# The last block's tail of a layer kernel: p's products kept on chip, W_G by blocks of k, weights split anew, one norm moved

## The chip, the cores and the metric

One Trainium2 chip, one core. The metric is the time of one execution on the device in microseconds (us); lower is better. A core has a matrix engine (PE, the tensor engine, with PEld for its weight loads), a vector engine (DVE), a scalar engine (ACT), a general engine (POOL) and SP, which issues transfers. Each works through its own queue in order; they meet at semaphores. Transfers (DMAs) issued by SP and POOL are carried out by 16 DMA engines. PE writes its sums to PSUM banks; all other tiles lie in SBUF; what is spilled lies in HBM.

## The reference

One layer is applied to 2048 prompt tokens and to 64 sample tokens. Only the part ahead of the output is touched by the change:

```python
merged = jax.nn.sigmoid(gA) * yA + jax.nn.sigmoid(gB) * yB
out = jnp.einsum('btd,de->bte', merged, w_o)
x = x + rms_norm(out, g_post)
gate = jax.nn.sigmoid(jnp.einsum('btd,de->bte', rms_norm(x, g_ple), w_ple_gate))
x = x + jnp.einsum('btp,pd->btd', p.astype(x.dtype), w_ple_proj) * gate
return x, new_conv, S_new
```

D_MODEL is 1024 and p has 256 columns. Everything is in float32.

## The kernel before

The 2112 tokens are cut into three blocks of BN = 704, and each block into two halves of HN = 352 (bl["segs"]). Activations lie feature by token: a tile `r` holds 128 features of a block, so eight tiles (KB = 8) make an operand. They come from one ring of 52 tiles (rt).

A float32 product is made of three matmuls in a shorter format: an operand is split into hi (rounded, cast by ACT, L184) and lo (the rest, subtracted by DVE, L185), and hi*hi, hi*lo and lo*hi are added in PSUM (mm3, L468 to L473, its three matmuls at L471, L472, L473). One output tile of 128 features by 352 tokens is thus 8 x 3 = 24 matmuls. split_w does the same for weights, which come as two halves of 128 x 512 each: the raw half is loaded by SP (L195). If its low part was kept in HBM by an earlier block, hi is cast by ACT (L215) and lo is loaded by SP (L216) into one of four tiles `lo` or three tiles `s`; otherwise lo is split by DVE (L185) into one of the four tiles `lo`. There are four tiles `hi` and five tiles `raw`.

In the last block, the stage W_O (out_in_turn) sums squares of its outputs, and its hooks already begin the norm of the first half. Then come:

- ple (L904 to L927): p times w_ple_proj, eight tiles of 2 x 6 matmuls (L918 to L920), copied from PSUM by ACT (L922) to a tile, which POOL spills (L924). After each tile a hook runs.
- final_gate (L1057 to L1069) for the first half, then for the second: per output tile j a product with W_G (gemm), a sigmoid (L1065), a reload of p by POOL (L931), multiply (L1066), add (L1067) and a store of y (L1068; on POOL, for j of 6 and 7 on SP). The reload brings all 704 columns for each half.

final_norm (L1020 to L1055) has 20 steps for one half: 2 for the reciprocal root of the mean square (sums by PE L558, scaling L530 on DVE, power on POOL L532, spread by PE L542, copied by ACT L568), 8 that scale, add x and square (L1040, L1041, L576, L577; x is loaded by POOL, L1032), 2 for the second root, and 8 that scale and split the operand of W_G (L1053, L184, L185). spread_out lays a list of counts over hooks: so many steps of a norm run at each hook. A framework schedules the instructions of one engine among each other from this order and from priorities, so that PE's matmuls of several output tiles can stand interleaved.

The hooks of the last block, before: the first norm runs 5 steps in W_O and 15 in the eight hooks of ple. The second norm runs 2 in ple (its first root) and 18 in the first seven hooks of the first half's gate.

Of the kernel before, what the change touches and what calls it, by code (L numbers as in the profile page):

```python
# [32 lines left out]
W_A, W_B, W_O, W_G = 80, 88, 96, 104  # L33
# [49 lines left out]
def hybrid_step(  # L83
# [17 lines left out]
    V, A, G, T, SP = nc.vector, nc.scalar, nc.gpsimd, nc.tensor, nc.sync  # L101
# [30 lines left out]
    def spill(kind, j):  # L132
        return dram.tile([P, BN], F32, tag=f"{kind}{j}", name=nm(kind), bufs=2)
# [76 lines left out]
    def split_w(raw, key=None):  # L210

        hi = wp.tile([P, 4, P], F32R, tag="hi", name=nm("hi"))
        if key in lows:
            lo = low_tile()
            A.copy(hi, raw)  # L215
            SP.dma_start(lo.bitcast(F32), lows[key])  # L216
            return hi, lo
        lo = wp.tile([P, 4, P], F32R, tag="lo", name=nm("lo"))
        split(raw, hi, lo)
        if key is not None:  # L220
            lows[key] = dram.tile([P, 4, P], F32, tag=f"lo{key}", name=nm("low"), bufs=1)
            SP.dma_start(lows[key], lo.bitcast(F32))
        return hi, lo

    def load_w(idx):

        parts = []
        for half_ in range(2):
            raw = load_raw(w_blk[idx, half_])
            with tc.high_priority():  # L230
                parts.append(split_w(raw, (idx, half_)))
        return parts

    last, hooks = [None], []
# [5 lines left out]
    def hook():  # L240

        if hooks:
            step = hooks.pop(0)
            if step is not None:
                step()
# [222 lines left out]
    def mm3(ps, w, act, k, c):  # L468
        hi, lo = w[k // 4]
        xhi, xlo = act[k]  # L470
        T.matmul(ps, hi[:, k % 4, :], xhi[:, c], start=k == 0, stop=False)  # L471
        T.matmul(ps, hi[:, k % 4, :], xlo[:, c], start=False, stop=False)  # L472
        last[0] = T.matmul(ps, lo[:, k % 4, :], xhi[:, c], start=False, stop=k == KB - 1).ins  # L473

    def cols_of(s):
        return slice(s["off"], s["off"] + s["n"])

    def gemm(idx, act, segs):
        w = load_w(idx)
        outs = []  # L480
        for s in segs:
            ps = ps_gemm()
            for k in range(KB):
                mm3(ps, w, act, k, cols_of(s))
            outs.append(ps)
            hook()
        return outs
# [10 lines left out]
                            mm3(ps, w, act, k, cols_of(s))  # L498
        return pss

    def gemm_by_k(idxs, act, segs):

        ws = [load_w(i) for i in idxs]
        pss = [[ps_gemm() for _ in segs] for _ in idxs]
        for k in range(KB):
            for row, w in zip(pss, ws):
                for ps, s in zip(row, segs):
                    mm3(ps, w, act, k, cols_of(s))
        return pss

    def gemms(idx0, act, segs, by_k=False):
# [394 lines left out]
    def ple(bl, ph, kept):  # L906
        for j in range(KB):
            raw = wp.tile([P, 4, P], F32, tag="raw", name=nm("raw"), bufs=5)[:, :2, :]
            SP.dma_start(raw, w_ple[j])
            with tc.high_priority():  # L910
                hi = wp.tile([P, 4, P], F32R, tag="hi", name=nm("hi"))[:, :2, :]
                lo = wp.tile([P, 4, P], F32R, tag="lo", name=nm("lo"))[:, :2, :]
                split(raw, hi, lo)
            t = rt()
            for s in bl["segs"]:
                pp, c = ps_attn()[:, :HN], cols_of(s)
                for k, (xhi, xlo) in enumerate(ph):
                    T.matmul(pp, hi[:, k, :], xhi[:, c], start=k == 0, stop=False)  # L918
                    T.matmul(pp, hi[:, k, :], xlo[:, c], start=False, stop=False)
                    last[0] = T.matmul(pp, lo[:, k, :], xhi[:, c], start=False, stop=k == 1).ins  # L920
                with tc.high_priority():
                    A.copy(t[:, c], pp)  # L922
            kept["p", j] = spill("p", j)
            G.dma_start(kept["p", j], t)  # L924
            hook()
            yield


    def reload(d):
        t = rt()  # L930
        G.dma_start(t, d)  # L931
        return t
# [121 lines left out]
            split(t[:, c], h2[j][0][:, c], h2[j][1][:, c])  # L1054
            yield  # L1055

    def final_gate(bl, segs, xo, h2, kept):  # L1057
        c = slice(segs[0]["off"], segs[-1]["off"] + HN)
        for j in range(KB):
            pss = gemm(W_G + j, h2, segs)  # L1060
            xj = reload(kept["x", j]) if ("x", j) in kept else xo[j]
            pj = reload(kept["p", j])
            t = rt()
            for s, ps in zip(segs, pss):
                A.activation(t[:, cols_of(s)], ps, AF.Sigmoid)  # L1065
            V.tensor_tensor(t[:, c], pj[:, c], t[:, c], ALU.mult)  # L1066
            V.tensor_tensor(t[:, c], t[:, c], xj[:, c], ALU.add)  # L1067
            (SP if bl["last"] and j >= KB - 2 else G).dma_start(y_fm[j * P : (j + 1) * P, segs[0]["t0"] : segs[0]["t0"] + len(segs) * HN], t[:, c])  # L1068
            yield  # L1069


    def spread_out(*plans):

        for counts in zip_longest(*(plan for _, plan in plans), fillvalue=0):
            todo = [(gen, n) for (gen, _), n in zip(plans, counts) if n]
            hooks.append((lambda todo=todo: [run(gen, n) for gen, n in todo]) if todo else None)
# [25 lines left out]
    for bi, bl in enumerate(blocks):  # L1102
        first, kept = bi == 0, kepts[bi]
        segs = bl["segs"]
        path_b(bl, hc, first, kept, fills)
        run(fills)
        a = []
        nxt = None if bl["last"] else blocks[bi + 1]
        cols, a_first = [], []
        rows = row_rstd(nxt, cols) if nxt else iter(())  # L1110
        sums_ahead = prepare_sums(W_A, W_B) if first else prepare_sums(W_O) if bi == 1 else iter(())

        def side(rows, sums_):
            for j in range(KB):
                if j <= 3:
                    next(rows, None)
                if j >= 3:
                    next(sums_, None)
                yield

        def ready():
            a_first.extend(narrow(half(t, 0)) for t in a[:KH])

        path_a(bl, hc, a, first, side(rows, iter(()) if first else sums_ahead), None if first else ready)
        assert not hooks
        if first:
            next(sums_ahead)
        mg, xo, h2, acc = [], [], [], rt()
        if first:
            mg = merge(bl, a, kept, sums_ahead)  # L1130
        else:
            parts = [None] * KB

            def made(j, h):

                if nxt:
                    if parts[j] is None:
                        parts[j] = rt(dt=F32R), rt(dt=F32R)
                    split(half(mg[j], h), *(half(t, h) for t in parts[j]))

            stages, loads = merge_in_turn(a, kept, mg, made)
            if not nxt:
                stages.append(out_in_turn(mg, xo, acc))
            loads(W_A, -1)
            for idx, n in in_turn(stages, a_first):
                loads(idx, n)
                if (idx, n) == (W_B, 5) and not nxt:
                    ph = [split_rt(raw) for raw in load_p(bl, G)]
                if (idx, n) == (W_O, 4):
                    norms = [final_norm(bl, [s], xo, acc, h2, None) for s in segs]  # L1150
                    spread_out((norms[0], (0, 0, 1, 0, 1, 1, 1, 1)))
            if nxt:
                mg = parts
        if nxt:
            hc = new_operands()
            ops = operands(hc, spread_all(cols), partial(load_x, nxt))
            for j, _ in enumerate(final_out(segs, mg, xo, acc, by_k=True)):
                if j in (1, 3, 5):
                    run(ops, 1)
            run(ops)  # L1160
            fills = gates(nxt, hc, kepts[bi + 1], False)
            norm = final_norm(bl, segs, xo, acc, h2, kept)
            spread_out((norm, (0, 1, 0, 1) + (0, 1, 0) * KB + (1, 0, 1) + (0, 1) * KB))
            run(fills, LEAD)
            assert not hooks
            run(final_gate(bl, segs, xo, h2, kept))
        else:
            gate = [final_gate(bl, [s], xo, h2, kept) for s in segs]
            spread_out((norms[0], (2, 2, 1, 1, 1, 3, 3, 2)), (norms[1], (0, 0, 1, 0, 1, 0, 0, 0) + (3, 3, 2, 1, 1, 4, 4)))
            run(ple(bl, ph, kept))  # L1170
            run(gate[0])
            assert not hooks
            run(gate[1])
# [49 lines left out]
```

## Time and profile before

| what | value |
|---|---|
| runs shown | 2727.76, 2730.09, 2732.46 us; median 2730.09 |
| the profiled execution | 2728.34 us |
| its span, first to last instruction | 2726.6 us |
| mean granted TensorE clock | 0.987 |
| PE busy in the span | 2646.6 us |
| DMA from 2640 to 2720 us | 25.95 MB, mean 324 GB/s |
| a cast of weights, ACT L215, 128 x 512 | 619 ns mean, 740 in the kernel |
| a split of weights, DVE L185, 128 x 512 | 660 ns mean |

The page calls each group of instructions by line, engine, operation and tile: "L347 PE MATMUL pg<-r,lo" is the matmul of line 347 that writes a PSUM tile pg and reads r and lo. In a list of waits, "PE pg L473 <- DMA s<-low: 1.7, 1, 1.7" says that PE's line 473 waited for a transfer to s, 1.7 us in all, once, 1.7 us the longest. In the timeline, a row is start, duration, engine, line, operation and tiles, and in brackets the idle time ahead of it with what ended it. Matmuls overlap: one that lasts 0.32 us lets the next start after 0.16 us. Starts are us from the first instruction.

### The profile page before, as it was taken

To read this page: it belongs to the slowest core of one execution; us is meant where nothing else is said; L and a number is where in the kernel's file an instruction comes from. 1 tells how busy PE (TensorE), PEld (TensorE's weight loads), DVE (VectorE), ACT (ScalarE), POOL (GpSimd) and SP (SyncE) were. 2 spreads that over 40 slices of the span, in tenths; PEclk is the share of its full clock that TensorE was granted. 3 is DMA by queue.
4 is the path that set the end of the run, shared out by engine and by line. 5 is a ranking of instruction groups with operands and counts; after the bars stand their busy time and mean duration, and the time that the engine had idled before them with its cause. 6 is when DMAs were issued, how large, how long until landed. Compare 5 with 4: busy or idle time off the path is not lost.

```text
span 2726.6 us, 47857 instructions
## 1 busy us (share of the span) xinstructions
PE 2646.6 (97%) x16736; PEld 2610.7 (96%) x16736; DVE 1721.8 (63%) x3327; ACT 1457.9 (53%) x2796; POOL 367.9 (13%) x684
## 2 busy tenths in 40 slices
PE   6999999999999999999999999999999999999998
PEld 5999999999999999999999999999999999999988
DVE  6788888899666643566645567554355554357864
ACT  4665565454324553566654556454466654445654
POOL 1000001100332211011111210021010010010022
PEclk7999999999999999999999999999999999999999
DMA  5767777898988898766789998598866678888878
GB/s 200 268 239 275 260 243 278 280 314 291 346 312 288 305 340 271 243 224 223 232 279 335 390 335 259 180 349 306 268 224 219 217 225 269 272 290 305 280 240 313
DMA packets 365681, 748.90 MB, mean 275 GB/s; under 512 B 44704, under 2 KB 48320, under 8 KB 365440
## 3 DMA queue, kind: packets, MB, share of 16 engines
q1 hardware_dynamic: 325728, 589.84, 64.9%
q0 software_dynamic: 39424, 155.96, 15.6%
q8 instruction: 132, 2.16, 0.3%
q14 instruction: 109, 0.89, 0.1%
q10 hardware_dynamic: 288, 0.05, 0.0%
HBM read 538.29 MB, written 207.37 MB: 273 GB/s over the span
## 4 chain that ended last, share of the span: by engine, by line
PE 78%; DMA 8%; DVE 4%; issue 4%; ACT 2%; POOL 1%; SPq 0%; DVEq 0%; POOLq 0%; ACTq 0%
PE pg L345 17%; PE pg L346 17%; PE pg L347 17%; PE pg L472 3%; PE pg L473 3%; PE pg L471 3%; PE pg L438 3%; PE pg L439 3%; PE pg L440 3%; DMA raw<-w_blk 2%; DMA raw<-S 1%; PE pa L826 1%; PE pa L862 1%; PE pa L864 1%; PE pa L816 1%
## 5 line engine op out<-in xcount | busy, mean ns | idle before, releaser
L345 PE MATMUL pg<-r,hi 128*128 128x352 f32 x3360 | 1115.1, 333 | 15.9 <-ACT r L184 5.9
L346 PE MATMUL pg<-r,hi 128*128 128x352 f32 x3360 | 1090.4, 325 | 5.0 <-DVE r L185 5.0
L347 PE MATMUL pg<-r,lo 128*128 128x352 f32 x2400 | 779.9, 325 | 4.8 <-DMA lo<-low 3.5
L215 ACT CAST hi<-raw 128x512 fp32r<-128x512 f32 x740 | 455.9, 619 | 589.7 <-PE pg L346 216.3
L345 PEld LDWEIGHTS pg<-r,hi 128*128 128x128 f32 x3360 | 634.8, 189 | 26.8 <-ACT r L184 8.9
L346 PEld LDWEIGHTS pg<-r,hi 128*128 128x128 f32 x3360 | 635.6, 189 | 9.6 <-DVE r L185 9.5
L347 PEld LDWEIGHTS pg<-r,lo 128*128 128x128 f32 x2400 | 454.0, 189 | 7.0 <-DMA lo<-low 4.7
L347 PE MATMUL pg<-r,s 128*128 128x352 f32 x960 | 310.5, 324 | 0.4 <-DMA s<-low 0.3
L472 PE MATMUL pg<-r,hi 128*128 128x352 f32 x896 | 291.9, 326 | 2.6 <-DVE r L185 2.3
L471 PE MATMUL pg<-r,hi 128*128 128x352 f32 x896 | 290.3, 326 | 1.8 <-ACT r L184 1.7
L473 PE MATMUL pg<-r,lo 128*128 128x352 f32 x728 | 237.5, 326 | 8.3 <-DVE lo L185 7.2
L184 ACT CAST r<-r 128x352 fp32r<-128x352 f32 (+2 forms) x294 | 162.8, 589 | 144.0 <-DVE r L962 43.3
L184 ACT CAST hi<-raw 128x512 fp32r<-128x512 f32 (+1 forms) x232 | 138.1, 597 | 181.2 <-PE pg L346 44.1
L185 DVE TENSOR_TENSOR r<-r,r 128x352 fp32r<-128x352 f32 (+2 forms) x294 | 183.6, 650 | 60.7 <-ACT r L184 60.0
L185 DVE TENSOR_TENSOR lo<-raw,hi 128x512 fp32r<-128x512 f32 (+1 forms) x232 | 152.2, 660 | 73.2 <-ACT hi L184 66.8
L438 PE MATMUL pg<-r,hi 128*128 128x352 f32 x560 | 182.6, 330 | 7.9 <-ACT r L184 7.9
L439 PE MATMUL pg<-r,hi 128*128 128x352 f32 x560 | 183.9, 330 | 0.9 <-DVE r L185 0.6
L347 PEld LDWEIGHTS pg<-r,s 128*128 128x128 f32 x960 | 180.4, 188 | 1.3 <-DMA s<-low 1.3
L472 PEld LDWEIGHTS pg<-r,hi 128*128 128x128 f32 x896 | 169.9, 190 | 4.5 <-DVE r L185 4.3
L184 ACT CAST hi<-s 128x512 fp32r<-128x512 f32 x160 | 98.8, 619 | 139.7 <-PE pg L346 137.0
L471 PEld LDWEIGHTS pg<-r,hi 128*128 128x128 f32 x896 | 169.6, 190 | 3.3 <-ACT r L184 2.9
L361 ACT COPY hf<-pg 128x352 f32<-128x352 f32 x360 | 158.3, 446 | 0.6
(327 smaller groups left out, 3991.7 us busy)
## 6 DMA issues: line engine op xcount, KB each, us to landing
raw<-w_blk SPq DMA_DIRECT2D x588, 256.0 KB, 4.0
lo<-low SPq DMA_DIRECT2D x422, 256.0 KB, 3.9
raw<-S SPq DMA_DIRECT2D x400, 256.0 KB, 4.0
low<-lo SPq DMA_DIRECT2D x344, 256.0 KB, 3.7
s<-low SPq DMA_DIRECT2D x318, 256.0 KB, 3.8
S<-s SPq DMA_DIRECT2D x160, 256.0 KB, 3.3
r<-x_fm POOLq DMA_DIRECT2D x40, 352.0 KB, 7.0
r<-w_blk POOLq DMA_DIRECT2D x48, 256.0 KB, 7.2
```

Of the source, the lines that this page charges most:

```text
L184: A.copy(hi, src)
L185: V.tensor_tensor(lo, src, hi.bitcast(F32), ALU.subtract)
L215: A.copy(hi, raw)
L345: add(hi[:, k, :], xhi, start=start and k == 0, stop=False)
L346: add(hi[:, k, :], xlo, start=False, stop=False)
L347: last[0] = add(lo[:, k, :], xhi, start=False, stop=k == KH - 1).ins
L361: copied = A.copy(got[n], ps[bank])
L438: add(hi[:, k, :], xhi, start=start and k == 0, stop=False)
L439: add(hi[:, k, :], xlo, start=False, stop=False)
L471: T.matmul(ps, hi[:, k % 4, :], xhi[:, c], start=k == 0, stop=False)
L472: T.matmul(ps, hi[:, k % 4, :], xlo[:, c], start=False, stop=False)
L473: last[0] = T.matmul(ps, lo[:, k % 4, :], xhi[:, c], start=False, stop=k == KB - 1).ins
```

## The change

For the last block alone:

1. ple keeps its eight tiles in SBUF (kept["p", j] = t): no spill, and final_gate takes the tile instead of reloading it.
2. final_gate makes its first two output tiles with gemm_by_k: both columns of W_G are loaded, and for each k the three matmuls of one and then of the other are given out, with a hook after every second k (four hooks for the pair). gemm_by_k is also used elsewhere, where no hooks are waiting.
3. The second half's gate loads its weights with anew=True: split_w gets no key, so lo is split by DVE and not loaded.
4. Of the second half's norm no step but the first two runs in ple, and these two in its last two hooks; 18 steps run in the ten hooks of the first half's gate (four of the pair, six of the rest).

```diff
-    def load_w(idx):
+    def load_w(idx, anew=False):
...
-                parts.append(split_w(raw, (idx, half_)))
+                parts.append(split_w(raw, None if anew else (idx, half_)))
...
-    def gemm_by_k(idxs, act, segs):
-
-        ws = [load_w(i) for i in idxs]
+    def gemm_by_k(idxs, act, segs, anew=False):
+
+        ws = [load_w(i, anew) for i in idxs]
         pss = [[ps_gemm() for _ in segs] for _ in idxs]
         for k in range(KB):
             for row, w in zip(pss, ws):
                 for ps, s in zip(row, segs):
                     mm3(ps, w, act, k, cols_of(s))
+            if k % 2:
+                hook()
         return pss
...
-            kept["p", j] = spill("p", j)
-            G.dma_start(kept["p", j], t)
+            if bl["last"]:
+                kept["p", j] = t
+            else:
+                kept["p", j] = spill("p", j)
+                G.dma_start(kept["p", j], t)
             hook()
...
-    def final_gate(bl, segs, xo, h2, kept):
+    def final_gate(bl, segs, xo, h2, kept, anew=False):
         c = slice(segs[0]["off"], segs[-1]["off"] + HN)
         for j in range(KB):
-            pss = gemm(W_G + j, h2, segs)
+            if not bl["last"]:
+                pss = gemm(W_G + j, h2, segs)
+            elif j == 0:
+                both = gemm_by_k([W_G, W_G + 1], h2, segs, anew)
+                pss = both[0]
+            else:
+                pss = both[1] if j == 1 else gemm(W_G + j, h2, segs, anew)
             xj = reload(kept["x", j]) if ("x", j) in kept else xo[j]
-            pj = reload(kept["p", j])
+            pj = kept["p", j] if bl["last"] else reload(kept["p", j])
...
-            gate = [final_gate(bl, [s], xo, h2, kept) for s in segs]
-            spread_out((norms[0], (2, 2, 1, 1, 1, 3, 3, 2)), (norms[1], (0, 0, 1, 0, 1, 0, 0, 0) + (3, 3, 2, 1, 1, 4, 4)))
+            gate = [final_gate(bl, [s], xo, h2, kept, anew=s is segs[1]) for s in segs]
+            spread_out((norms[0], (2, 2, 1, 1, 1, 3, 3, 2)), (norms[1], (0,) * 6 + (1, 1) + (2, 2, 2, 2, 1, 1, 2, 2, 2, 2)))
```

(gemm takes and hands on anew in the same way.)

## The prediction

> **What bounds the kernel now.** I read the page first (span, engines), then the waits of the tensor engine from 2630 us on, then that stretch cut into stages, then the tile p, and last the rows of four places in order of time. The built programs hold the same instructions in the same order on every engine up to about 2630 us: all that the change does lies in the last 97 us.
>
> ```profile
> span 2726.6 us, 47857 instructions
> PE 2646.6 (97%) x16736; PEld 2610.7 (96%) x16736; DVE 1721.8 (63%) x3327; ACT 1457.9 (53%) x2796; POOL 367.9 (13%) x684
> ```
>
> TensorE (PE) is the bound with 97%; only its idle stretches, its slow stretches and what follows its last matmul can be won. Of those after 2630 us, in total and longest:
>
> ```profile
> PE pg L473 <- DMA s<-low: 1.7, 1, 1.7
> PE pg L472 <- DVE r L185: 1.5, 1, 1.5
> PE pg L473 <- DMA lo<-low: 1.1, 1, 1.1
> PE pa L918 <- DVE cols L530: 0.5, 2, 0.3
> PE pg L471 <- ACT r L184: 0.4, 1, 0.4
> ```
>
> Two are low parts of weights that land late, two are operands of the second half that are made late. (The 3.8 us wait at L918, 2626.3 to 2630.1, is in both programs.) By stage: start:end, length, busy of PE, PEld, DVE, ACT, POOL, granted clock, DMA share, GB/s:
>
> ```profile
> 2630.00:2647.00 17.00, 16.39 (x98) 16.15 (x99) 11.79 (x29) 11.15 (x27) 6.99 (x11) 0.91 0.73 238
> 2647.00:2687.00 40.00, 37.12 (x226) 35.19 (x224) 25.52 (x53) 22.16 (x48) 11.08 (x20) 1.00 0.95 341
> 2687.00:2720.00 33.00, 30.83 (x176) 29.72 (x176) 11.10 (x22) 12.00 (x25) 9.07 (x17) 0.95 0.87 309
> ```
>
> W_G runs with the transfers at 0.95 and 0.87 of their engines; VectorE is free for 22 of the last 33 us. The tile p, spilled and reloaded, holds VectorE up:
>
> ```profile
> L931 POOL DMA_DIRECT2D r<-p x16: 536/536/541, 2658.0 to 2717.9; - x16
> L924 POOL DMA_DIRECT2D p<-r x8: 539/544/600, 2630.7 to 2655.9; - x8
>   DVE r L1066: 26.3, 10
> DMA to landing us min/median/max: 2.5/5.5/7.9
> ```
>
> The second half's first matmuls, in order of time, then the granted clock (second last number) of a stretch just behind them:
>
> ```profile
> 2686.57 0.32 PE L471 MATMUL pg<-r,hi 128*128 128x352 f32 x1
> 2688.38 0.43 PE L472 MATMUL pg<-r,hi 128*128 128x352 f32 x1 [1.49 <-DVE r L185]
> 2691.25 0.49 PE L471 MATMUL pg<-r,hi 128*128 128x352 f32 x1
> ...
> 2691.30:2694.60 3.30, 3.30 (x13) 3.30 (x12) 0.08 (x1) 0.98 (x2) 0.41 (x1) 0.50 0.98 375
> ```
>
> And the end; the last matmul began at 2719.57 and ended at 2719.89:
>
> ```profile
> 2719.93 0.46 ACT L1065 ACTIVATE r<-pg 128x352 f32<-128x352 f32 x1 [3.38 <-PE pg L473]
> 2720.73 0.53 DVE L1066 TENSOR_TENSOR r<-r,r 128x352 f32<-128x352 f32 x1 [3.72 <-DMA r<-p]
> 2722.02 0.53 DVE L1066 TENSOR_TENSOR r<-r,r 128x352 f32<-128x352 f32 x1 [0.20 <-DMA r<-p]
> 2722.58 0.52 DVE L1067 TENSOR_TENSOR r<-r,r 128x352 f32<-128x352 f32 x1
> ```
>
> The last product of p lands 1.5 us after its sigmoid.
>
> **The change part by part.** A matmul of 352 columns starts 0.16 us after the one before it where nothing waits (rows at 2688.65 and 2688.82). "Lost" below is the time between two starts less 0.16 us for each matmul.
>
> *p's products kept.* Eight spills and 16 reloads of 352 KB go (8.65 MB), with the 24 issues of 0.54 us on POOL, behind which y_fm's stores stood. *Weights split anew:* 16 loads of 256 KB go from SP's queue (4.2 MB). Of the 26 MB that the DMA view counts from 2640 to 2720 us these are nearly half. What is late for want of it: at 2648.94 a matmul waited for lo, issued 2644.04; at 2667.32 for s, issued 2659.88, 7.4 us before. From 2604 to 2622, with 226 GB/s moving, the same loads of 256 KB landed after 2.7 to 3.4 us. That would be 2647.4 and 2663.3, both before their matmuls were due (2647.7, 2665.5). Lost there: 2647.55 to 2649.21 took 1.66 for two matmuls, so 1.34; 2665.31 to 2667.59, 1.96. Gain 3.3 us; bounds 0 (it lands as late as now) and 3.3.
>
> The 16 splits cost VectorE 16 x 0.66 us (row L185, lo<-raw,hi, 128x512) in a stage where it is busy 11.1 of 33 us. A column of 24 matmuls lasts 3.87 us; its two splits and its multiply and add are 2 x 0.66 + 2 x 0.53 = 2.4 us of VectorE, its two casts (0.62) and sigmoid 1.7 us of ScalarE. In the built order a column's splits stand ahead of the multiply two columns before it, so they hide behind a column of matmuls: 0 us. The cast is the same work at L184 instead of L215. If that cover went, a split is 0.66 us per half column.
>
> *That half's norm later.* It leaves ple (L558 sums, L530, one pow, two matmul spreads) and the operands of the first half: eight L1040 no longer stand between the eight L1053, whose rows then follow each other every 1.58 us (2653.82, 2655.40, 2656.97). Now the chain runs from 2643.6 to 2659.1; then it takes 8 x 1.58 = 12.6 us from about 2641.1, to 2653.7. PE gets there after three columns of ple (5.8 us), the small matmuls (1.4) and six groups of k for two columns (5.8): 2640.4 + 13 = 2653.4. I take 0.3 us of waiting there; bounds 0 and 1.5 (ScalarE's casts of weights stand between those of operands). In ple two waits of 0.26 for L530 give way to one before the L558 of the first half: its last add ends at 2637.08 (L1041 at 2635.49, square 2636.03 to 2636.53, add 0.52), PE is there at 2636.44: 0.65 for 0.5, with the slower restarts (0.27 instead of 0.16) 0.03 lost.
>
> Inside the first half's gate the whole norm now runs: eight x loads, 23 VectorE operations and eight squares ahead of its second sum, 16 and eight casts behind it. From that sum to its spread PE has little to do: before, L558 began at 2671.04 and L542 at 2673.09, and eight matmuls filled that; in the built order three do. 2.05 - 0.69 (L558) - 0.48 = 0.88 us lost; bounds 0.7 and 1.4.
>
> Does the second half then start without waiting? PE reaches that L558 at 2630.11 + 198 matmuls (31.7) + half clock (1.5) + small matmuls (2.7) + waits (1.1) = 2667.1. From L558 to the end of the copy (L568) it is 3.46 us now: 2670.6. The first operand is there 1.6 us later, the eighth after 12.6 us, 2683.2; at most 2689.9, if five multiplies and adds (4.4) and four splits (2.3) do not fit into VectorE's waits for casts ([0.55 <-ACT r L184] in the rows). PE begins the second half at 2669.2 + 0.7 + 75 matmuls (12.0) = 2681.9, and, two columns by blocks of k, needs the eighth operand 14 groups of three later, 2688.6. So the wait goes, with 1.3 us as its worst. Lost now: nine matmuls from 2686.57 to 2691.25 took 4.68 us, so 3.24. Gain 3.24.
>
> *The clock.* From 2691.25 to 2694.66 matmuls start every 0.29 us at a granted 0.50, right behind those waits: 3.41 x (1 - 0.16/0.29) = 1.53 us. The other rows at 0.50 also follow stalls (2630 after 3.8 us). I take the gain, 1.53; bounds 0 and 1.53. The Trainium skill ("TensorE: Matmul & The Clock Gate", Part 1) has the clock fall only after an idle window of about 3.4 us, free-running; the row fell after waits that sum to less, and a 1.68 us wait at 2665.6 left it at 1.00. By that rule the fall has another cause and stays, and the gain is 1.5 us smaller.
>
> *W_G's first two columns by blocks of k.* PE now already interleaves its first three columns as operands come, and loses about 0.84 us there in pitches of 0.21 to 0.34. Two columns by k should lose about half: gain 0.4, bounds 0 and 0.84.
>
> *The end.* After the last matmul: sigmoid 0.46, multiply 0.53, add 0.53 with 0.03 between, store issued at once, and from issue (2723.13) to the end of the span 3.47. That is 5.1 us instead of 2726.6 - 2719.89 = 6.7. Gain 1.6; nothing hides it.
>
> Sum: 3.3 + 3.24 + 1.53 - 0.03 - 0.3 - 0.88 + 0.4 + 1.6 = 8.8 us. The profiled execution took 2728.34 us, its span 2726.6: 2719.5 and 2717.8. The three runs shown have a median 1.75 us above it, 2730.09: so 2721.3 us. About 0.2% (5.5 us) is what a measurement of this kernel can tell from no change.
>
> **The rivals.** (1) *The second half still waits:* its x loads need ring tiles of which eight now hold p, or its casts stand behind those of weights. Then 3.24 + 1.53 stay: 2721.3 + 4.8 = 2726.1, within 0.2%. For it: the whole norm must fit into 31 us. Against: the 6.7 us of spare above. (2) *Transfers are as late as now,* because raw weights, x and y still come in bursts: 3.3 us stay, 2724.6. For it: 0.95 of the DMA engines busy. Against: half of the bytes go. (3) *Slower:* the splits of a column come to VectorE only behind the multiply of the column just before. Then its third matmul waits for sigmoid, multiply, add and split, 0.5 + 0.53 + 0.53 + 0.66 - 0.32 = 1.9 us in each of six columns, and at 1.9 us in every 5.8 the clock may fall each time (1.53): 6 x 3.4 = 20.6, 2741.9. It decides from 2.4 us a column. For it: SP no longer brings lo, and VectorE works strictly in order. Against: the built order has the splits two columns ahead. (4) *The half clock has another cause* than the waits and comes anyway: 1.53 us stay, 2722.8. For it: the 1.68 us wait that left the clock at 1.00. Against: the other rows at 0.50 stand behind stalls. The Trainium skill's rule above speaks for it.
>
> **How the numbers follow.** Forecast 0.69, (1) 0.10, (2) 0.09, (3) 0.05, (4) 0.07. The forecast's own range: the runs spread by 2.4 us to either side, and the small bounds by 1.5: 2717 to 2726. The range reaches on to (1) and (2) with that spread: 2716.5 to 2728. Faster by over 0.2% (below 2724.6): most of the forecast and of (4), half of (2), a third of (1): 0.75. Within: 0.20. Slower by over 0.2%: (3), 0.05.
>
> **What would show it.** In the profile after: no wait of PE for lo or s behind 2630 us; no stretch at 0.50 near 2680; a wait of about 0.9 us for POOL at the second spread, in the fifth column of the first half; a first L473 of the second half that waits for nothing; about 5 us from the last matmul to the end. It is wrong if PE waits for DVE lo in the second half, or if the span is above 2722.

## The result, and the profile after

| | before | after |
|---|---|---|
| median, us (runs) | 2731.28 (6) | 2719.90 (6) |
| lowest to highest, us | 2727.76 to 2738.80 | 2717.64 to 2724.43 |
| ratio of after to before | | 0.9958, 95% interval 0.9945 to 0.9971 |
| the profiled execution, us | 2728.34 | 2724.43 |
| its span, us | 2726.6 | 2722.7 |

The change takes 0.42% (0.29 to 0.55%) off. The profiled execution of after happens to be the slowest of its six. So totals of two profiled executions mislead here (3.9 us apart, where the medians are 11.4 us apart), and the study measures a stretch instead. Up to the 3.8 us wait in ple all kernels have the same order of matmuls (the last kernel below shortens that wait, and is measured from an earlier one); **the tail** is the time from the release of that wait to the end of the span. In before it runs from 2630.11 to 2726.6, 96.5 us; in after from 2635.88 to 2722.7, 86.8 us. The tail is 9.7 us shorter.

The page of after, span and engines:

```profile
span 2722.7 us, 47814 instructions
PE 2643.6 (97%) x16736; PEld 2609.2 (96%) x16736; DVE 1729.7 (64%) x3343; ACT 1457.2 (54%) x2796; POOL 354.2 (13%) x660
```

The same number of matmuls; POOL has 24 instructions fewer (the spills and reloads of p), VectorE 16 more (the splits). The waits of TensorE in the tail (the lines have moved: 918 and 922 became 920 and 924, the sum of a norm at 558 became 560, the spread at 542 became 544, scaling 530 became 532, sigmoid, multiply, add and store 1065 to 1068 became 1076 to 1079):

```profile
PE pa L920 <- ACT r L924: 3.8, 1, 3.8
PE pa L544 <- POOL cols L534: 0.8, 1, 0.8
PE pa L560 <- DVE r L579: 0.5, 1, 0.5
```

The first is the wait that opens the tail. Of the waits of before (lo, s, the second half's operands, 4.7 us in all, and two of 0.25 us in ple) none is left; two new ones of 0.83 and 0.52 us have come. By stage (length, busy of PE, PEld, DVE, ACT, POOL, granted clock, DMA share, GB/s):

```profile
2635.88:2652.88 17.00, 16.48 (x97) 16.07 (x98) 11.09 (x26) 12.01 (x29) 2.59 (x4) 0.91 0.44 131
2652.88:2685.00 32.12, 31.29 (x197) 30.38 (x196) 26.28 (x56) 20.01 (x43) 7.78 (x14) 1.00 0.82 270
2685.00:2718.30 33.30, 33.30 (x208) 33.04 (x206) 21.04 (x40) 13.10 (x26) 3.24 (x6) 1.00 0.43 138
```

The third line is the second half's gate: TensorE is never idle and the clock never falls, the transfers need 0.43 of their engines instead of 0.87, VectorE has 21 us of work instead of 11. And the end, from the last matmul:

```profile
2718.01 0.32 PE L473 MATMUL pg<-r,lo 128*128 128x352 f32 x1
2718.37 0.46 ACT L1076 ACTIVATE r<-pg 128x352 f32<-128x352 f32 x1 [3.40 <-PE pg L473]
2718.87 0.53 DVE L1077 TENSOR_TENSOR r<-r,r 128x352 f32<-128x352 f32 x1 [2.78 <-ACT r L1076]
2719.43 0.53 DVE L1078 TENSOR_TENSOR r<-r,r 128x352 f32<-128x352 f32 x1
2719.98 0.34 SPq L1079 DMA_DIRECT2D y_fm<-r  x1
```

The multiply follows the sigmoid at once; nothing waits for a transfer.

### The profile page after: what moved, and what is told of

The parts are those of the page before. It is cut to its first block, busy times and chain, and to the rows that moved or that the text cites. A ratio compares the mean times of both kernels' runs of the same rounds, so it can differ in the third digit from the quotient of the medians.

```text
span 2722.7 us, 47814 instructions
## 1 busy us (share of the span) xinstructions
PE 2643.6 (97%) x16736; PEld 2609.2 (96%) x16736; DVE 1729.7 (64%) x3343; ACT 1457.2 (54%) x2796; POOL 354.2 (13%) x660
## 4 chain that ended last, share of the span: by engine, by line
PE 79%; DMA 7%; issue 5%; DVE 4%; POOL 2%; ACT 1%; SPq 0%; DVEq 0%; POOLq 0%; ACTq 0%
PE pg L345 17%; PE pg L346 17%; PE pg L347 17%; PE pg L472 4%; PE pg L473 4%; PE pg L471 4%; PE pg L438 3%; PE pg L439 3%; PE pg L440 3%; DMA raw<-w_blk 2%; DMA raw<-S 2%; PE pa L828 1%; PE pa L864 1%; PE pa L866 1%; PE pa L818 1%
## 5 line engine op out<-in xcount | busy, mean ns | idle before, releaser
L215 ACT CAST hi<-raw 128x512 fp32r<-128x512 f32 x724 | 445.8, 619 | 571.8 <-PE pg L346 215.2
L184 ACT CAST hi<-raw 128x512 fp32r<-128x512 f32 (+1 forms) x248 | 147.8, 598 | 195.3 <-PE pg L472 41.1
L185 DVE TENSOR_TENSOR r<-r,r 128x352 fp32r<-128x352 f32 (+2 forms) x294 | 183.5, 649 | 62.1 <-ACT r L184 61.4
L185 DVE TENSOR_TENSOR lo<-raw,hi 128x512 fp32r<-128x512 f32 (+1 forms) x248 | 162.6, 660 | 81.3 <-ACT hi L184 72.8
```

The source lines that it names most:

```text
L184: A.copy(hi, src)
L185: V.tensor_tensor(lo, src, hi.bitcast(F32), ALU.subtract)
```

## The experiments

Twelve kernels ran; eleven stand in the table with before and after, the twelfth comes last. "PE" is the tail up to the last matmul's end; the waits are those of TensorE in the tail of 0.4 us or more; the last column is the stretch at a granted clock of 0.50 behind them (every kernel has one more, of 3.41 us, at the start of the tail).

| kernel | tail, PE (us) | waits (us) | at 0.50 | ratio to before, 95% |
|---|---|---|---|---|
| before | 96.5, 89.8 | 1.08, 1.68, 1.49, 0.42 | 3.41 | |
| after | 86.8, 82.5 | 0.52, 0.83 | - | 0.9958 (0.9945-0.9971) |
| p alone | 92.7, 88.4 | 2.76 | 6.83 | 0.9986 (0.9976-0.9996) |
| all but p | 92.2, 87.8 | 0.41, 2.78, 0.42, 0.43 | 3.41 | 0.9971 (0.9962-0.9981) |
| all but the splits | 86.9, 82.5 | 0.51, 0.83 | - | 0.9963 (0.9949-0.9977) |
| all but the later norm | 87.5, 83.2 | 0.67 | - | 0.9962 (0.9948-0.9976) |
| p and columns by k | 87.5, 83.2 | 0.67 | - | 0.9957 (0.9943-0.9970) |
| p and splits | 93.1, 88.7 | 2.94 | 6.83 | 0.9967 (0.9954-0.9980) |
| p, one store on SP | 88.2, 83.4 | 0.68 | - | 0.9967 (0.9954-0.9979) |
| after, splits in both halves | 93.6, 89.3 | 0.42, 4.70 | 6.83 | 0.9984 (0.9972-0.9996) |
| after once more | 86.8, 82.5 | 0.41, 0.83 | - | 0.9950 (0.9933-0.9967) |
| all but columns by k | 86.6, 82.2 | 0.42, 0.81 | - | 0.9944 (0.9931-0.9956) |
| p and the later norm | 86.4, 82.0 | 0.43, 0.84 | - | 0.9957 (0.9943-0.9970) |

The tail of one kernel came out the same twice (after, 86.8 and 86.8), while the totals have intervals of 2.6 to 4.6 us to either side: verdicts below rest on the tails and the waits. A tail is that of one traced execution, though, so where a total and a tail disagree, this is said.

### p alone

```diff
 # in before
-            kept["p", j] = spill("p", j)
-            G.dma_start(kept["p", j], t)
+            if bl["last"]:
+                kept["p", j] = t
+            else:
+                kept["p", j] = spill("p", j)
+                G.dma_start(kept["p", j], t)
...
-            pj = reload(kept["p", j])
+            pj = kept["p", j] if bl["last"] else reload(kept["p", j])
```

> The kernel before with p's products kept on chip and nothing else of the change. Tail = from the release of the long wait in ple (2630.1 us before, 2635.9 after) to the span's end: 96.5 us before, 86.8 after. Theory A, the prediction's sum, each part its own term: p brings the end (1.6) and its share by bytes of the late landings (8.65 of 12.85 MB, 2.2 of 3.3): tail 92.7, ratio 0.9986; the second half still waits for operands. Theory B: p's reloads stood behind nearly all of it, since VectorE's multiplies waited for them and so did the second half's norm behind them: tail 87 to 88.5, ratio 0.997, no wait of more than 0.5 us at the second half's first matmuls.

Measured: tail 92.7 us, exactly theory A's number, and not by theory A's mechanism. The waits of TensorE in its tail (here the sum of a norm is L558, its add L577):

```profile
PE pa L918 <- ACT r L922: 3.8, 1, 3.8
PE pa L558 <- DVE r L577: 2.8, 1, 2.8
PE pa L918 <- DVE cols L530: 0.3, 1, 0.3
```

No wait for lo or s, although all lows are loaded, and none for the second half's operands, although the norm runs as before: both had gone with p alone. In their place stands one new wait, at the sum of the second half's norm. What is late there is seen in the timeline, first in POOL's rows:

```profile
2658.67 0.54 POOL L1035 DMA_DIRECT2D r<-x_fm  x1 [1.47 <-PE pa L919]
2672.62 0.54 POOL L1071 DMA_DIRECT2D y_fm<-r  x1 [13.41 <-DVE r L1070]
2673.15 0.54 POOL L1035 DMA_DIRECT2D r<-x_fm  x1
```

and then in VectorE's, where L1070 is the add of an output, L1044 adds x and L577 adds its square:

```profile
2675.66 0.52 DVE L1070 TENSOR_TENSOR r<-r,r 128x352 f32<-128x352 f32 x1
2678.80 0.52 DVE L1044 TENSOR_TENSOR r<-r,r 128x352 f32<-128x352 f32 x1 [2.62 <-DMA r<-x_fm]
2679.89 0.53 DVE L577 TENSOR_TENSOR r<-r,r 128x352 f32<-128x352 f32 x1 [0.56 <-ACT r L576]
```

The last of the norm's eight x_fm loads is queued on POOL behind the first store of y; the store waits for VectorE, POOL is idle for 13.41 us, and the load goes out at 2673.15. It lands at 2678.78, and x is added, squared and summed only then. In before and in after no x_fm load stands behind a store of y. Two causes were left: the load's place in the queue, and its 5.63 us to land.

The second half starts some 5 us later here than in the kernels without this wait, which gives VectorE time for its operands. That p alone removes the waits for lo, s and the operands even without this delay is seen further down, in p with one store on SP.

### All but p

The changed kernel, with p's products spilled and reloaded as in before:

```diff
 # in after
-            if bl["last"]:
-                kept["p", j] = t
-            else:
-                kept["p", j] = spill("p", j)
-                G.dma_start(kept["p", j], t)
+            kept["p", j] = spill("p", j)
+            G.dma_start(kept["p", j], t)
...
-            pj = kept["p", j] if bl["last"] else reload(kept["p", j])
+            pj = reload(kept["p", j])
```

> The changed kernel with p spilled and reloaded again, the other three parts kept. Theory A: the end (1.6) and 2.2 us of late landings come back: tail 90.6, ratio to before 0.9978. Theory B: VectorE waits for p again, the second half's operands and the splits of its weights stand behind those waits: tail 92 or more, with waits of PE on VectorE in the second half.

Measured: 92.2 us, as theory B had it. The cause of its 2.78 us wait can be read from ScalarE's rows:

```profile
2665.37 0.50 ACT L578 ACTIVATE r<-r 128x352 f32<-128x352 f32 x1 [0.79 <-DVE r L1043]
2668.98 0.62 ACT L215 CAST hi<-raw 128x512 fp32r<-128x512 f32 x1 [3.12 <-DMA raw<-w_blk]
2669.51 0.88 ACT L578 ACTIVATE r<-r 128x352 f32<-128x352 f32 x2
```

ScalarE stands 3.12 us at a cast of weights whose raw half has not landed, and two squares of the norm (L578), whose inputs are ready by 2667.6, wait behind it; the sum for which TensorE waits until 2671.24 needs them. The transfers issued from 2655 to 2669 in this kernel (count, size, median from issue to landing):

```profile
DMA packets 2194, 5.04 MB, mean 360 GB/s; under 512 B 319, under 2 KB 319, under 8 KB 2193
...
raw<-w_blk SPq DMA_DIRECT2D x6, 256.0 KB, 9.0
r<-x_fm POOLq DMA_DIRECT2D x6, 176.0 KB, 6.0
s<-low SPq DMA_DIRECT2D x3, 256.0 KB, 8.6
lo<-low SPq DMA_DIRECT2D x3, 256.0 KB, 9.2
r<-p POOLq DMA_DIRECT2D x2, 352.0 KB, 7.9
p<-r POOLq DMA_DIRECT2D x1, 352.0 KB, 5.5
```

In after the same stretch behind the wait in ple (2658.8 to 2672.8) has raw weights landing after a median of 5.0 us. So spilling p does make weights late, as the prediction said: what arrives late is raw, and the norm pays, not the product. Of p itself only three transfers lie in this stretch; the six x_fm loads lie in it too, since POOL issues them behind p's last spill (2655.26), while in after all eight are out before it. Which of the two weighs more was not tried. The splits cannot help here: SP issues lows of the first half up to 2670.30, and the 4.2 MB that they spare would come behind that. And theory B had the number, but put the waits into the second half: there stand only the two of 0.42 and 0.43 us.

### All but the splits, and all but the later norm

```diff
 # in after: all but the splits
-            gate = [final_gate(bl, [s], xo, h2, kept, anew=s is segs[1]) for s in segs]
+            gate = [final_gate(bl, [s], xo, h2, kept, anew=False) for s in segs]
 # in after: all but the later norm
-            ... (norms[1], (0,) * 6 + (1, 1) + (2, 2, 2, 2, 1, 1, 2, 2, 2, 2))
+            ... (norms[1], (0, 0, 1, 0, 1, 0, 0, 0) + (3, 3, 2, 1, 1, 4, 4))
```

> The changed kernel with the low parts of the second half's weights loaded again. Theory A: a third of the late landings comes back, 1.1 us: tail 87.9. Theory B: with p's bytes gone the loads land in time: tail 86.8, within 0.4; PE waits for no low part in the second half.

> The changed kernel with the second half's norm at its old hooks (its first root early in ple, 18 steps in the first seven hooks of the gate). Theory A: the waits of the second half and the half clock come back, 4.8 less the 0.9 of the spread: tail about 90.7. Theory B: without p's reloads that norm is in time at either place: tail 87 to 88, no wait over 0.5 us at the second half's first matmuls.

Measured: 86.9 and 87.5 us, as theory B had it. Neither part is missed by more than 0.7 us when it is taken out alone.

### p with one other part, and p with one store moved

Which part keeps the wait of p alone away? Three kernels: p with columns by k and nothing else; p with the splits and nothing else; and p alone with this edit, which touches the place of the load only:

```diff
 # in p alone
-            (SP if bl["last"] and j >= KB - 2 else G).dma_start(y_fm[...], t[:, c])
+            (SP if bl["last"] and (j >= KB - 2 or j == 0 and segs[0]["off"] == 0) else G).dma_start(y_fm[...], t[:, c])
```

> Before, with two parts of the change: p's products kept, and W_G's first two columns by blocks of k; lows loaded in both halves, the norm spread as before. In p kept alone, TensorE waited 2.76 us at the sum of the second half's norm, and 6.83 us at half clock followed: the last x_fm load of that norm was issued by POOL at 2673.15, behind a y_fm store that waited for VectorE until 2671.8, and landed 5.63 us later. Theory P (its place): p's eight tiles hold ring tiles, so this load comes behind the first store of y in POOL's queue; the columns by k put all eight loads ahead of it. Then no wait over 0.7 us at that sum, nothing at 0.50 behind it, and from the release of the 3.8 us wait to the end of the span 87.5 +- 0.7 us (p kept alone: 92.7; after: 86.8). Theory T (the traffic): it waits because loads land after 5 to 6 us as long as the lows are loaded; then a wait of 1.5 us or more stays, and 90 us or more.

> Before, with p's products kept and the second half's weights split anew (4.2 MB less to load), and nothing else. The last x_fm load of the second half's norm stands behind the first y_fm store in POOL's queue, as in p kept alone. Theory P (its place): the wait at that norm's sum stays at 2 us or more, and the tail (from the release of the 3.8 us wait to the end of the span) is 91 to 93 us, ratio about 0.9985. Theory T (the traffic): with the lows gone the load lands within 3.4 us of its issue instead of 5.63, the wait falls to 0.5 us, no half clock follows, and the tail is 87.4 to 89 us, ratio about 0.9965.

> p kept alone, with one edit: the first half's first y_fm store goes by SP's queue instead of POOL's, so that the last x_fm load no longer stands behind it; as many bytes as before, lows loaded, no columns by k, the norm as before. Theory P (its place): no wait over 0.7 us at the sum of the second half's norm, no stretch at 0.50 there, tail 86.9 to 88.5 us (92.7 without the edit), ratio about 0.996. Theory T (the traffic): the wait stays at 1.5 us or more and the tail at 90 us or more. If SP's queue now stands still behind the store, the next raw weights land late and TensorE waits for a cast or a low part instead: a wait for DMA or for hi names it.

Measured: tails of 87.5, 93.1 and 88.2 us, theory P in all three. The total of p with the splits is not: its ratio is 0.9967, where theory P had 0.9985 and theory T 0.9965. Two of its seven executions took 2716.5 and 2717.9 us, the other five 2724.1 to 2726.4; the trace is of one of the five, and what the two did differently is open. By totals alone this kernel and p with one store on SP (0.9967 too) cannot be told apart. With the first store on SP, POOL's timeline reads

```profile
2655.00 1.06 POOL L1035 DMA_DIRECT2D r<-x_fm  x2 [1.47 <-PE pa L919]
2672.83 0.54 POOL L1071 DMA_DIRECT2D y_fm<-r  x1 [16.76 <-DVE r L1070]
```

The last load, one of the two at 2655.00, now goes out 17 us ahead of the next store; as many bytes are moved as in p alone, and the wait of 2.76 us is gone. The second half then waits for nothing, with the norm where it was before. In p with the splits POOL's timeline has the load behind the store as in p alone, and it lands 5.8 us later:

```profile
2664.79 0.55 POOL L1071 DMA_DIRECT2D y_fm<-r  x1 [13.41 <-DVE r L1070]
2665.33 0.54 POOL L1035 DMA_DIRECT2D r<-x_fm  x1
```

This kernel is a weaker test of the traffic than its expectation says. Its last low of the first half goes out at 2667.51, and nearly all of the 4.2 MB that the splits spare would come later: from the load's issue to its landing 1.77 MB were moved, against 1.93 MB in p alone. That the place decides rests on the store moved to SP and on the columns by k.

The price of the place can be added up: p alone has a tail 5.2 us longer than p with columns by k, 2.1 us for the longer wait (2.76 against 0.67) and about 1.5 us for each of its two windows at 0.50. Why the order comes out so when p is kept is not settled: p's eight tiles hold ring tiles that the loads could have had, and y is ready sooner because it waits for no reload. For the first speaks that in p alone the three loads ahead of the last wait too, for an add, a split and a matmul of ple (L919, in the first of its POOL rows above); a larger ring was not tried.

### The splits in both halves

```diff
 # in after
-            gate = [final_gate(bl, [s], xo, h2, kept, anew=s is segs[1]) for s in segs]
+            gate = [final_gate(bl, [s], xo, h2, kept, anew=True) for s in segs]
```

> The changed kernel with the weights split anew in the first half of W_G too: 16 more splits of 0.66 us on VectorE, 16 loads of 256 KB fewer. The first half's gate has the second half's norm and operands on VectorE, so the cover that the second half has is thin there. Theory S (the cover is gone): TensorE waits 3 us or more for casts and splits in the first half's gate, tail 90 to 93 us (after: 86.8), ratio about 0.998. Theory H (a split always hides behind a column of matmuls of 3.9 us): no new wait over 0.5 us, tail 86.8 +- 0.5 us, ratio as after, 0.9958.

Measured: 93.6 us, theory S and a little more. The wait does not stand where the theory put it. TensorE's list of waits:

```profile
PE pg L471 <- ACT r L1076: 4.7, 1, 4.7
```

ScalarE's timeline just ahead of it:

```profile
2674.95 0.93 ACT L578 ACTIVATE r<-r 128x352 f32<-128x352 f32 x2 [1.45 <-DVE r L1046]
2676.76 0.50 ACT L578 ACTIVATE r<-r 128x352 f32<-128x352 f32 x1 [0.87 <-DVE r L1046]
2677.16 1.15 ACT L1076 ACTIVATE r<-pg 128x352 f32<-128x352 f32 x3
```

And VectorE's, which has a split (L185) just ahead of the add (L1046):

```profile
2673.80 0.69 DVE L185 TENSOR_TENSOR lo<-raw,hi 128x512 fp32r<-128x512 f32 x1
2674.40 0.95 DVE L1046 TENSOR_TENSOR r<-r,r 128x352 f32<-128x352 f32 x2
```

TensorE waits for no low part but for a PSUM bank: three sigmoids, which empty the banks, stand on ScalarE behind squares of the norm, and these wait for VectorE (L1046), which does the splits in between. In the second half no norm is left, and the 16 splits cost nothing. The prediction's slower rival also has splits in VectorE's way, but in the second half, by another chain (its matmul waits for the low part) and at another price (20.6 us; here the tail is 6.8 us longer).

### The rest

The changed kernel once more:

> The changed kernel once more, nothing edited. Theory P (the tail is fixed by the queues' orders): the tail (from the release of the 3.8 us wait to the end of the span) is again 86.8 +- 0.4 us, with waits of about 0.5 us at the second sum of the first half's norm and 0.83 us for POOL. The spans of the ten kernels so far differ by up to 18 us though; theory C (the clock) says that most of that lies ahead of the tail, in stretches at 0.50: the clock is set anew every 3.41 us, on a grid that runs free of the program, and is 0.50 in the window after one in which TensorE was idle for more than about 1.7 us (in ten profiles, 84 of 84 windows with 1.8 us or more idle, 10 of 7,700 with less than 1.0 that follow a window at full clock or not). Then here too every window with 1.8 us or more idle is followed by 0.50, and next to none with under 1.2 us; a rival theory, that the clock falls only after a whole idle window of 3.41 us, allows a fall at no more than a handful of places.

Measured: 86.8 us and waits of 0.41 and 0.83, as expected; its span is 2715.6, that of the first profile 2722.7. Nearly all of this lies ahead of the tail (2628.78 against 2635.88). The clock is taken up in the last section, where the windows are counted over all fourteen profiles; those counts replace the ones in this expectation.

All but the columns by k, and p with the later norm alone:

```diff
 # in after, both kernels
-            elif j == 0:
+            elif j == 0 and False:
...
-                pss = both[1] if j == 1 else gemm(W_G + j, h2, segs, anew)
+                pss = gemm(W_G + j, h2, segs, anew)
...
-            ... (norms[1], (0,) * 6 + (1, 1) + (2, 2, 2, 2, 1, 1, 2, 2, 2, 2))
+            ... (norms[1], (0,) * 6 + (1, 1) + (4, 4, 1, 1, 2, 2, 2, 2))
 # p with the later norm: also anew=False
```

> The changed kernel without the columns by k: W_G's first two columns one after the other, the second half's norm at (0,)*6+(1,1)+(4,4,1,1,2,2,2,2), as late as in the change. All eight x_fm loads of that norm still stand ahead of the first y_fm store in POOL's queue. Theory P (the columns by k matter by the order of those loads alone): no wait over 1 us behind the 3.8 us wait, tail 86.3 to 87.5 us, ratio as after, 0.9958. Theory K (they matter by themselves, since the first column then needs the eighth operand after 2.9 us of matmuls and not after 5.8): waits for operands or casts at the start of the first half's gate of 1.5 us or more in sum, tail 88.5 us or more.

> Before, with two parts: p's products kept, and the second half's norm as late as in the run without columns by k; no columns by k, lows loaded in both halves. All eight x_fm loads of that norm stand ahead of the first y_fm store in POOL's queue. Theory P (p kept, and an order in which no x_fm load stands behind a store of y; nothing else is needed): tail 86.4 to 87.2 us, no wait over 1 us behind the 3.8 us wait, ratio about 0.995. Theory A (each part has a term of its own, the weights split anew about 1 us for the transfers): 87.9 us or more, with a wait for lo or s.

Measured: 86.6 and 86.4 us; theory P twice. Two of the four parts do all of it.

Last, an attempt to beat both:

```diff
 # in after
-                    spread_out((norms[0], (0, 0, 1, 0, 1, 1, 1, 1)))
+                    spread_out((norms[0], (0, 0, 1, 0, 1, 0, 0, 0)))
...
-            spread_out((norms[0], (2, 2, 1, 1, 1, 3, 3, 2)), (norms[1], (0,) * 6 + (1, 1) + (2, 2, 2, 2, 1, 1, 2, 2, 2, 2)))
+            spread_out((norms[0], (1, 1, 2, 2, 2, 3, 4, 3)), (norms[1], (0,) * 6 + (1, 1) + (1, 1, 2, 2, 2, 2, 2, 2, 2, 2)))
```

(The recorded text says that the first half's norm begins earlier. In the list for W_O three of its steps are taken out, and in ple the three are spread over later hooks, so most of it comes later; the waits it names are those of this edit.)

> The changed kernel with the first half's norm begun earlier and the second half's two k-blocks later: its steps are taken at the fifth column of W_O and in ple by (1,1,2,2,2,3,4,3) instead of (2,2,1,1,1,3,3,2), so that the 3.79 us wait in ple for the copy of the spread falls apart into waits of about 0.8, 1.8 and 1.4 us. Measured from the third wait of over 0.6 us near 2465 us (the last before the stretch that differs) to the end of the span, the changed kernel took 251.1 us (before 260.9). Theory S (the stall is shortened, the rest stays): 249.2 us, and 247.7 if the stretch at 0.50 behind that wait goes too; it stays if the waits of 1.8 and 1.4 us fall into one window of 3.41 us. Ratio to before about 0.995, to the changed kernel 0.999. Theory D (the chain of that norm ends no earlier, since VectorE and ScalarE are what it waits for): 251 us, ratio as after.

Measured: 251.3 us (after 251.1, after once more 252.2), waits of 0.61, 1.80 and 1.22 us, a stretch at 0.50 behind them, ratio 0.9957 (0.9944 to 0.9969): theory D. The waits from there on sum to 4.3 us instead of 5.1; that small difference does not show in the time. No kernel of the twelve beats the changed one by more than the intervals.

## Why the prediction came true, and where its steps did not

**The sum.** The forecast was 2721.3 us, the median of after 2719.9; the forecast sum of 8.8 us (the terms as written give 8.9) is to be held against 9.7 us of tail. Up to the last matmul it was 8.9 - 1.6 = 7.3 us, and 89.8 - 82.5 = 7.3 was measured. That the two agree to a tenth is luck: two terms of 0.3 and 0.4 us with opposite signs were both about zero. The medians of the totals lie 11.4 us apart; 1.7 us of that are not in the tail.

**Late lo and s, 3.3 us.** Gone, as predicted. But the step gave the credit to p and to the splits together ("nearly half" of the bytes). P alone, with every low loaded, has no such wait, and the splits add nothing that can be seen (86.9 against 86.8). Nor could they: the two waits end at 2648.94 and 2667.32, both in the first half. After, which loads lows for the first half alone, issues 13 of them behind the wait in ple; in before the 13th and the 14th from that wait on are

```profile
2669.23 0.33 SPq L216 DMA_DIRECT2D s<-low  x1
...
2671.15 0.33 SPq L216 DMA_DIRECT2D lo<-low  x1
```

So every load that the splits spare is issued behind both waits, and their 4.2 MB did not belong in this step. Whether p's bytes or its place in the queues made lo and s late was not separated.

**The second half's operands, 3.24 us.** Gone, as predicted, and again by another part than the one named. The prediction put it to the norm moved later, with its 6.7 us of spare. In p alone and in p with one store on SP the norm runs as before, and the second half waits for nothing; without p, with the norm moved, two waits of 0.42 and 0.43 us stay. VectorE works in order, and without the reloads, for which it had waited 26.3 us at L1066 in before, operands are no longer queued behind a waiting multiply. This is a reading of the rows; the runs show that p decides.

**The half clock, 1.53 us.** Gone from the second half in all kernels without a long wait there, and back behind every wait of 2.76 us or more. Rival 4 (another cause) has fallen. The Trainium skill ("TensorE: Matmul & The Clock Gate", Part 1) gives a free-running window of about 3.4 us, and the grid of 3.41 us agrees. Its condition, a whole idle window, does not: no wait here but the one in ple is that long, apart from one of 4.70 us in one experiment, and the clock fell all the same.

**The wait for POOL, 0.88 us, and the first sum of ple, 0.65 (0.5 before).** 0.83 (twice) and 0.41 to 0.52 measured, at the predicted places. The 0.3 us of operand waits in the first half did not come.

**Columns by k, 0.4 us.** Without them the tail is 86.6 instead of 86.8: nothing, within its bounds (0 to 0.84). Where they do matter, with p kept and the norm as before (87.5 against 92.7), it is by the order on POOL: they put the x_fm loads ahead of the stores.

**The end, 1.6 us.** Mis-sized: from the last matmul's end to the end of the span it went from 6.75 to 4.37 us, 2.4 us. The multiply's wait accounts for the 1.6; the rest lies behind the store's issue (3.5 us before, 2.7 after).

**The rivals.** Rival 1 (the second half waits, because kept tiles take ring tiles from the x loads) is false of the change. P alone comes near it: a late x_fm load, at a cost of 2.76 us and a stretch at 0.50 of 6.83 us, but the wait stands in the first half's gate, and the ring as its reason is not shown. Rival 2 (transfers as late as now) is false: from 2640 to 2720 us raw weights land after a median of 3.0 us instead of 6.3. Rival 3 is false of the change: TensorE waits for no split. Splits in the first half do cost time, by another chain. Of the signs of error that were named, one appears: the profiled span is above 2722. It was a badly chosen sign, since the second profile of the same kernel spans 2715.6.

The step that failed is thus the apportioning, not the sum: the prediction took four parts for four gains, and the runs show one gain (p's 24 transfers) and one condition (no x_fm load behind a store of y on POOL) that the columns by k, the later norm or one store moved to SP fulfils.

## What to carry to other kernels

A buffer kept on chip can reorder what competes for its space or waited for its reload: look at each in-order queue for a load that now stands behind a store, and try moving that one store before paying for anything larger. Take the parts of a bundled change out one at a time and put them in one at a time: four parts seemed to have a term each, and two of them (the splits, and either the columns by k or the later norm) added nothing that can be seen. And when a run hits a theory's number, look at its waits before believing the theory: p alone hit 92.7 us with none of the waits that the theory had summed.

## What the runs showed of the hardware

**The clock follows windows of 3.41 us, half idle is enough.** All stretches at 0.50 start on a grid of 3.41 us and last multiples of it, but for one that the end of the program cuts off. Two pairs of windows of this grid in before (columns as in the stages above):

```profile
2663.95:2667.36 3.41, 1.73 (x12) 1.44 (x10) 2.76 (x6) 2.01 (x5) 1.19 (x3) 1.00 1.01 362
2667.36:2670.77 3.41, 3.41 (x21) 3.41 (x22) 1.48 (x4) 1.58 (x4) 0.93 (x2) 1.00 1.06 401
...
2687.84:2691.25 3.41, 2.19 (x8) 1.37 (x9) 2.38 (x6) 1.62 (x4) 2.19 (x5) 1.00 0.92 286
2691.25:2694.66 3.41, 3.41 (x14) 3.41 (x13) 0.14 (x1) 0.98 (x2) 0.47 (x1) 0.50 0.99 380
```

And four in a row of p alone:

```profile
2676.72:2680.13 3.41, 0.99 (x7) 0.69 (x5) 0.77 (x2) 0.77 (x3) 0.30 (x1) 1.00 0.99 357
2680.13:2683.55 3.42, 3.05 (x11) 2.60 (x12) 2.27 (x6) 0.95 (x3) 1.36 (x2) 0.50 0.68 228
2683.55:2686.96 3.41, 3.41 (x14) 3.41 (x15) 1.46 (x4) 1.55 (x4) 0.84 (x2) 0.50 0.29 106
2686.96:2690.37 3.41, 3.41 (x23) 3.41 (x22) 3.13 (x8) 2.41 (x6) 0.54 (x1) 1.00 0.73 230
```

In p alone TensorE is busy for 0.99 of 3.41 us, the next window is at 0.50, and the one after it too, although TensorE idled for only 0.37 us of the first. In before it is idle for 1.68 us (busy 1.73) and the clock stays, and for 1.22 us (busy 2.19) and the clock falls, so the idle time of one window does not decide by itself near the bound. Counted over the fourteen profiles from 60 us on, by the idle time of TensorE in a window: of windows at full clock with under 1.0 us idle, 5 of 10,543 are followed by one at 0.50; with 1.0 to 1.4 us, 1 of 68; with 1.4 to 1.8 us, 12 of 25; with 1.8 us or more, 75 of 75. Of windows at 0.50 with 0.4 us idle or more, 74 of 81 are followed by another; with less, 3 of 103, of which the one above is one. So a wait of about 2 us costs itself and, depending on where the grid falls, some 1.5 us more per window behind it: such a window holds 14 matmuls instead of 23, at 0.16 us each.

**Executions differ by where the grid falls.** Over the fourteen profiles the start of the last stage (2461.5 to 2473.9 us, the same work in all) goes with the time at 0.50 from 80 us to there (18 to 36 us) with a correlation of 0.85 and 0.56 us for each microsecond. Much of the spread between executions of one kernel is therefore of this kind; that it is all of it was not shown.

**Late landings had a margin here.** In the 14 us that start 22.9 us behind the wait in ple the raw weights land after a median of 5.0 us in after and of 4.3 us in p with columns by k, and no wait of TensorE comes of either. In all but p it is 9.0 us, and TensorE waits 2.78 us for the norm's sum. Where between 5 and 9 us the margin ends was not measured.
